# A depthwise convolution on TensorE: 128x128 diagonals replaced by 32x32 diagonals in sixteen tiles of the array

## The chip, the cores and the metric

The kernel runs on one core of one Trainium2 chip. The metric is the device time of one execution in microseconds (us); the figure quoted for a kernel is the median of several runs. TensorE (PE in the profile) has its matmuls and its weight loads (PEld) on separate rows, VectorE is DVE, ScalarE is ACT, GpSimd is POOL, and SP issues the DMAs.

## What is computed

The program is a trunk of four pre-norm residual layers on 256 tokens of 1024 features, in float32. Each layer has a token mixer and a gated feed-forward network (FFN) with a short convolution. The mixers are differential attention (layers 0 and 3), a Conformer convolution module (layer 1) and a gated DeltaNet (layer 2). The change touches the Conformer module and the FFN that stands ahead of it:

```
u = h @ w_in + b_in                       # 1024 -> 2048
a, g = split(u); u = a * sigmoid(g)
u = causal_dwconv(u, dw) + dw_b           # 31 taps, each channel by itself
mu = mean(u); var = mean((u - mu)**2)     # over the 1024 channels
u = (u - mu) * rsqrt(var + 1e-5) * ln_g + ln_b
return silu(u) @ w_out + b_out
```

## The kernel before, in words

Features lie on the 128 partitions and the 256 tokens along the free dimension, so 1024 channels are eight blocks, b = 0 to 7. Weights stream from HBM as units of 128x1024 float32; each unit is split by ACT (`whi`, L173) and DVE (`wlo`, L174) into two float32r halves, and every product with a weight is three float32r matmuls (`mm3`, L282 to L284).

The Conformer module (`conformer`) runs a software pipeline over b. `glu(b)` makes both halves of the gated projection, 48 matmuls of 128x128 by 128x256 into the PSUM tile `pcu`; `glu_act` then has DVE scale them (`cs`, L695), ACT take the sigmoid (`csg`, L697) and DVE form `cu` (L700), the block's convolution input with 30 zero columns ahead of it. `conv(b)` shares out the 31 taps:

- TensorE takes the first 10 (11 in the last block). Each tap is a float32 matmul of a 128x128 diagonal `dg` with the shifted `cu`, which the chip runs as two passes, so 20 matmul instructions of 256 columns in `pcc` (L712). The diagonals are made by ACT (`diag`, L650); `some_diags` puts up to 88 of them into the FFN ahead, four per step of it, and all of the 81 that are needed fit.
- The next six are multiplied by ACT (`ct`, L728) and added by GpSimd into `ya` (L729); from b = 2 on, GpSimd also subtracts the shift `m0` (L731).
- Taps 29 and 30 are ACT's (L724, L725), and the other 13 are DVE's fused multiply-adds (`tap`, L722), accumulated in a PSUM tile `cyp`. Two DVE adds join the parts to `c[:, b]` (L735, L736), and ACT squares the block (L750).

`stat(b)` sums `c` and its square over the channels with TensorE: four passes of a 128x1 weight into `pstat` (L757) for each block, in the middle of the next block's taps. For b = 6 the sums are copied out and turned over to tokens (L763, L765), and for b = 7 they are added token by token (L760). `shift` (L743) takes the mean of block 0 as an early shift, so that the later difference of squares keeps its digits; its matmul stands behind the taps of block 1. After `stat(7)` follow the mean and the reciprocal deviation (L781 to L789), eight activations and the output projection `acc`.

Each engine runs its own instructions in the order that the build put them in. On TensorE that is the order of the calls: glu(b), conv(b - 1), glu(b + 1). On DVE, ACT and GpSimd the work of neighbouring blocks interleaves.

Of the kernel before, what the change touches and what calls it, by code (L numbers as in the profile page):

```python
# [12 lines left out]
ALU = mybir.AluOpType  # L13
# [17 lines left out]
N_RAW = 4  # L31
PE_TAPS = 10
PE_TAPS_LAST = 11
POOL_TAPS = 6
LAG = 2
AT_X, AT_R, AT_S, AT_F, AT_A, AT_C, AT_G = 7, 3, 10, 0, 0, 4, 2
MAX_DIAGS = 88
DIAG_STEP = 4
TAIL = 4
# [42 lines left out]
C_ID, C_LE, C_GT, C_ONE, C_HALF = 0, P, 2 * P, 3 * P, 3 * P + P  # L82
N_CONST = C_HALF + 16

# [41 lines left out]
def trunk(ctx: ExitStack, tc: tile.TileContext, xT, pos, wst, wba, params, consts, rows, lamp, nfin, out, layers=None):  # L126
# [11 lines left out]
    def bank(name="ps"):  # L138
        return wk.tile([P, 512], F32, name=name, tag="wk")
# [55 lines left out]
    neg_half = cst[:, C_HALF:C_HALF + 16]  # L195
    one_col = tri_le[:, P - 1:P]

    def col(name, i):
        c = COLS[name] + i
        return prm[:, c:c + 1]  # L200
# [444 lines left out]

    diags = {}

    def diag(dg, b, j):

        ac.activation(dg, ident, AF.Copy, scale=col("conv_dw", b * 31 + j))  # L650

    def some_diags(pool):

        for n, (b, j) in enumerate((b, j) for b in range(KC) for j in range(pe_taps(b))):
            if n == MAX_DIAGS:
                return
            dg = diags[b, j] = pool.tile([P, P], F32, name=f"dg{b}_{j}")
            diag(dg, b, j)
            if n % DIAG_STEP == DIAG_STEP - 1:
                yield  # L660

    def pe_taps(b):
        return PE_TAPS if b < KC - 1 else PE_TAPS_LAST

    def conformer(after):
        with ExitStack() as es:
# [3 lines left out]
            c = one.tile([P, KC, S], F32, name="cc")  # L670
            pstat = accp.tile([P, 2, 512], F32, name="pstat", tag="acc01")
            psum, ptok = pstat[:, 0], pstat[:, 1]
            m0 = one.tile([P, S], F32, name="m0")
# [3 lines left out]

            def glu(b):
                ps = bank("pcu")
                if b == 0:  # L680
                    pair_proj(ps, nxt(2))
                    norm_stat()
                    us[0] = ps
                    return
                for gv in range(2):
                    feat_proj(ps[:, gv * S:(gv + 1) * S], nxt()[0])
                    if b == 1 and gv == 0:
                        row_bc(rs_tok, rs_bc)
                if b == 1:
                    glu_act(0, us.pop(0))  # L690
                glu_act(b, ps)
# [10 lines left out]

            def conv(b):
                u = us.pop(b)
                npe = pe_taps(b)
                pc = bank("pcc")
                for n, j in enumerate(range(npe)):
                    dg = diags.pop((b, j), None)
                    if dg is None:
                        dg = pool.tile([P, P], F32, name="dg", bufs=6)  # L710
                        diag(dg, b, j)
                    pe.matmul(pc[:, 0:S], dg, u[:, j:j + S], start=(n == 0), stop=(n == npe - 1))  # L712
                    if n == npe - 1 and b == 1:
                        shift()
                    if n == npe // 2 and b > 2:
                        stat(b - 1)
                npo = npe + POOL_TAPS
                ya, yc = (pool.tile([P, S], F32, name=f"cy{n}") for n in range(2))
                acc = accp.tile([P, 2, S], F32, name="cyp", tag=f"acc{2 + b % 2}")

                def tap(j, out, y, op=ALU.add):
                    ve.scalar_tensor_tensor(out, u[:, j:j + S], col("conv_dw", b * 31 + j), y, ALU.mult, op)  # L722

                ac.activation(ya, u[:, 30:], AF.Identity, scale=col("conv_dw", b * 31 + 30), bias=col("conv_dw_b", b))  # L724
                ac.activation(yc, u[:, 29:29 + S], AF.Copy, scale=col("conv_dw", b * 31 + 29))  # L725
                for j in range(npe, npo):
                    t = pool.tile([P, S], F32, name="ct", bufs=3)
                    ac.activation(t, u[:, j:j + S], AF.Copy, scale=col("conv_dw", b * 31 + j))  # L728
                    gp.tensor_tensor(ya, ya, t, ALU.add)  # L729
                if b > 1:  # L730
                    gp.tensor_tensor(ya, ya, m0, ALU.subtract)  # L731
                tap(npo, acc[:, 0], yc)
                for j in range(npo + 1, 29):
                    tap(j, acc[:, 0], acc[:, 0])
                ve.tensor_tensor(yc, acc[:, 0], ya, ALU.add)  # L735
                ve.tensor_tensor(c[:, b], pc[:, 0:S], yc, ALU.add)  # L736
                if b > 1:
                    square(b)

            def shift():  # L740
# [5 lines left out]
            def square(b):  # L746
                if b < 2:
                    ve.tensor_tensor(c[:, b], c[:, b], m0, ALU.subtract)
                sqs[b] = pool.tile([P, S], F32, name="csq", bufs=3)
                ac.activation(sqs[b], c[:, b], AF.Square)  # L750

            def stat(b):

                both = (c[:, b], sqs.pop(b))
                if b < KC - 1:
                    for n, x in enumerate(both):
                        pe.matmul(psum[0:1, n * S:(n + 1) * S], ones_n[:, 0:1], x, start=(b == 0 and n == 0), stop=(b == KC - 2 and n == 1))  # L757
                else:
                    for n in range(4):
                        pe.matmul(ptok[:, n:n + 1], both[n // 2][:, n % 2 * P:(n % 2 + 1) * P], ones_n[:, 0:1], start=False, stop=(n == 3))  # L760
                if b == KC - 2:
                    row = one.tile([1, 512], F32, name="crow")
                    ac.copy(row, psum[0:1])  # L763
                    for n in range(4):
                        pe.matmul(ptok[:, n:n + 1], row[:, n * P:(n + 1) * P], one_col[0:1], start=(n == 0), stop=False)  # L765

            for b in range(KC + 1):
                if b < KC:
                    glu(b)
                if b >= 1:  # L770
                    conv(b - 1)
                if b == 2:
                    square(0)
                    square(1)
                if b == 3:
                    stat(0)
                    stat(1)
            stat(KC - 1)
            tk = one.tile([P, 2], F32, name="ctk")
# [560 lines left out]
    for k, (i, s) in enumerate(layers):  # L1340
        if s:
            extra = iter(())
            if k + 1 < len(layers) and layers[k + 1][0] % 3 == 1 and not layers[k + 1][1]:
                cdiag = ExitStack()
                extra = some_diags(cdiag.enter_context(tc.tile_pool(name="cdiag", bufs=1)))
            ffn(i, after_of(k), extra, k + 1 == len(layers))
# [24 lines left out]
def pack(inp, layers=None):  # L1371
# [100 lines left out]
    cst[:, C_ONE:C_ONE + P] = 1.0 / D  # L1472
    cst[:, C_HALF:] = -0.5

# [27 lines left out]
```

## Time and profile before

| | us |
|---|---|
| median of 3 runs | 1384.86 |
| lowest and highest run | 1383.97, 1385.96 |
| the profiled execution, its own time | 1386.96 |
| its span | 1385.1 |
| PE, DVE, ACT, POOL busy in the span | 1363.5, 1110.9, 879.9, 94.9 |

The profile is one execution. Its own time is 1.9 us more than its span and 2.1 us more than the median. A row of the timeline gives the start, the time from the first start to the last end, the engine, line, operation, output and inputs; in brackets stands the idle time ahead of it and what ended it. Matmuls overlap one another, so the pace of a stream is read from starts, not from the length of one.

### The profile page before, as it was taken

Reading aid. Unit: us, or ns where it says so; the run is one execution under the profiler, and the core shown is the slowest. Engines: PE = TensorE matmul, PEld = TensorE weight load, DVE = VectorE, ACT = ScalarE, POOL = GpSimd, SP = SyncE. Lnnn points to the kernel's source line nnn. Section 1 sums busy time; section 2 is a strip of 40 time slices with the busy share of each in tenths; the row PEclk is TensorE's granted clock in tenths of the full one; section 3 lists DMA queues with packets and bytes.
Section 4 is the critical chain, followed back from the end, with each engine's and each line's share of the span. In section 5 each row is a group of like instructions: output and inputs, shape, how many; then the busy total and the mean of one; then the engine's idle time right before and its main releaser. Section 6 shows DMA issues by size and latency. Waiting matters only on the chain.

```text
span 1385.1 us, 27575 instructions
## 1 busy us (share of the span) xinstructions
PE 1363.5 (98%) x10868; PEld 1292.5 (93%) x10868; DVE 1110.9 (80%) x1994; ACT 879.9 (64%) x1621; POOL 94.9 (7%) x112
## 2 busy tenths in 40 slices
PE   9999999999999999999999999999999999999998
PEld 7889999998889999998989999999999988999996
DVE  7977877788988877787994886797778786787776
ACT  6668965576656555575747765665556576655554
POOL 0010000004530000000100011000000000000000
PEclk9999999999999999999998999999999999999999
DMA  8445666654315666663462333566666544566662
GB/s 281 149 123 158 185 191 188 193 183 122 96 58 171 198 189 192 185 181 122 137 184 91 123 92 110 160 191 185 192 187 184 183 127 133 162 204 186 193 185 91
DMA packets 63138, 223.94 MB, mean 162 GB/s; under 512 B 7200, under 2 KB 8736, under 8 KB 63008
## 3 DMA queue, kind: packets, MB, share of 16 engines
q1 hardware_dynamic: 62720, 221.65, 52.5%
q8 instruction: 85, 1.39, 0.4%
q10 hardware_dynamic: 288, 0.52, 0.1%
q14 instruction: 45, 0.37, 0.1%
HBM read 221.10 MB, written 1.05 MB: 160 GB/s over the span
## 4 chain that ended last, share of the span: by engine, by line
PE 84%; DVE 9%; ACT 4%; POOL 1%; issue 1%; DMA 0%; SPq 0%; POOLq 0%; ACTq 0%; DVEq 0%
PE psu L282 11%; PE psu L283 11%; PE psu L284 11%; PE acc L282 8%; PE acc L283 8%; PE acc L284 8%; DVE wlo L174 3%; PE pgc L282 2%; PE pcc L712 2%; PE pgc L283 2%; PE pgc L284 2%; ACT whi L173 2%; PE pz L282 1%; PE pz L283 1%; PE pz L284 1%
## 5 line engine op out<-in xcount | busy, mean ns | idle before, releaser
L174 DVE TENSOR_TENSOR wlo<-wraw,whi 128x1024 fp32r<-128x1024 f32 (+1 forms) x417 | 508.8, 1222 | 134.6 <-ACT whi L173 132.6
L173 ACT CAST whi<-wraw 128x1024 fp32r<-128x1024 f32 (+1 forms) x417 | 436.0, 1047 | 272.9 <-PE psu L283 105.8
L282 PE MATMUL psu<-xh,whi 128*128 128x256 f32 x1344 | 375.9, 280 | 0.0
L283 PE MATMUL psu<-xl,whi 128*128 128x256 f32 x1344 | 375.2, 279 | 0.0
L284 PE MATMUL psu<-xh,wlo 128*128 128x256 f32 x1344 | 375.1, 279 | 0.0
L282 PEld LDWEIGHTS psu<-xh,whi 128*128 128x128 f32 x1344 | 252.6, 188 | 0.4
L283 PEld LDWEIGHTS psu<-xl,whi 128*128 128x128 f32 x1344 | 252.6, 188 | 0.4
L284 PEld LDWEIGHTS psu<-xh,wlo 128*128 128x128 f32 x1344 | 252.6, 188 | 0.0
L282 PE MATMUL acc<-facth,whi 128*128 128x256 f32 x528 | 147.6, 280 | 0.0
L283 PE MATMUL acc<-factl,whi 128*128 128x256 f32 x528 | 147.3, 279 | 0.0
L284 PE MATMUL acc<-facth,wlo 128*128 128x256 f32 x528 | 146.9, 279 | 0.0
L426 DVE SCALAR_TENSOR_TENSOR fy<-fs,prm,fy 128x255 f32<-128x255 f32 (+1 forms) x352 | 146.4, 477 | 0.0
L422 ACT ACTIVATE fy<-fs,prm 128x256 f32<-128x256 f32 x176 | 96.4, 593 | 8.3 <-DVE fs L418 8.3
L282 PEld LDWEIGHTS acc<-facth,whi 128*128 128x128 f32 x528 | 99.2, 188 | 0.2
L283 PEld LDWEIGHTS acc<-factl,whi 128*128 128x128 f32 x528 | 99.2, 188 | 0.0
L284 PEld LDWEIGHTS acc<-facth,wlo 128*128 128x128 f32 x528 | 99.0, 188 | 0.0
L276 ACT CAST facth<-fa 128x256 fp32r<-128x256 f32 x88 | 35.7, 405 | 93.0 <-DVE fa L430 92.8
L418 DVE TENSOR_TENSOR fs<-psu,rs_bc 128x512 f32<-128x512 f32 x88 | 60.7, 690 | 27.5 <-PE psu L284 26.8
L282 PE MATMUL pqk<-xh,whi 128*128 128x256 f32 x256 | 72.7, 284 | 0.0
L284 PE MATMUL pqk<-xh,wlo 128*128 128x256 f32 x256 | 72.3, 282 | 0.4 <-DVE wlo L174 0.4
L283 PE MATMUL pqk<-xl,whi 128*128 128x256 f32 x256 | 72.4, 283 | 0.0
L282 PE MATMUL pgc<-xh,whi 128*128 128x256 f32 x240 | 69.6, 290 | 0.0
(352 smaller groups left out, 2874.7 us busy)
## 6 DMA issues: line engine op xcount, KB each, us to landing
wraw<-wst SPq DMA_DIRECT2D x415, 512.0 KB, 3.7
h<-xT SPq DMA_DIRECT2D x4, 256.0 KB, 5.0
prm<-params SPq DMA_DIRECT2D x1, 564.0 KB, 7.4
wraw<-wst SPq DMA_DIRECT2D x2, 256.0 KB, 4.0
gain<-nfin SPq DMA_DIRECT2D x1, 512.0 KB, 4.7
out<-fz SPq DMA_DIRECT2D x2, 256.0 KB, 2.0
out<-fz ACTq DMA_DIRECT2D x2, 256.0 KB, 2.5
cst<-consts SPq DMA_DIRECT2D x1, 264.0 KB, 7.5
```

The costliest lines, as they stand in the source:

```text
L173: ac.copy(hi[:, qs], src[:, qs])
L174: ve.tensor_tensor(lo[:, qs], src[:, qs], hi[:, qs].bitcast(F32), ALU.subtract)
L276: state["hi"] = ac.copy(hi, a)
L282: pe.matmul(o, w[0], x[0], start=start, stop=False)
L283: pe.matmul(o, w[0], x[1], start=False, stop=False)
L284: pe.matmul(o, w[1], x[0], start=False, stop=stop)
L418: ve.tensor_tensor(s, ps.rearrange("p (g t) -> p g t", g=2), bc(rs_bc, 2), ALU.mult)
L422: ac.activation(y[:, gv], s[:, gv], AF.Identity, scale=col("ffn_dw", c + 2), bias=col("ffn_dw_b", (i * NP_ + p) * 2 + gv))
L426: ve.scalar_tensor_tensor(y[:, gv, j:], s[:, gv, :S - j], col("ffn_dw", c + 2 - j), y[:, gv, j:], ALU.mult, ALU.add)
L712: pe.matmul(pc[:, 0:S], dg, u[:, j:j + S], start=(n == 0), stop=(n == npe - 1))
```

## The change

TensorE gets 16 taps of each block (20 of the last), GpSimd four in place of six, and DVE nine (five in the last). The diagonal of a tap is kept as four 32x32 diagonals, one for each 32-partition group: `tap_blocks` makes all taps of a block with one GpSimd multiply of a stack of four 32x32 identities (new in `cst`) with the tap columns of `prm`. `some_taps` does that in the FFN ahead, one block at every second step, in place of ACT's 81 diagonals.

A group of four taps runs as 16 small matmuls: row group i of the array reads partitions 32i to 32i+31 of `cu`, column group j holds tap 4r+j, and the result goes to PSUM bank i, partitions 32j to 32j+31. So a bank holds, for 32 channels, four partial sums over taps, one on each partition quarter. ACT copies the four banks to SBUF (`cysb`, three copies), and `join(b)` adds the four quarters by four matmuls with the identity stack, each into one partition quarter of `pcc`. `join(b)` stands between the two halves of glu(b + 2).

DVE's taps accumulate in `yc` in SBUF, since the PSUM banks of `cyp` now hold the partial sums. The sums for the norm over blocks 0 to 6 are made by GpSimd (`total`, two adds a block), and TensorE turns them over to tokens once, after `join(6)`; `join(7)` stands behind that. `shift` moves to `join(0)`.

```diff
-PE_TAPS = 10
-PE_TAPS_LAST = 11
-POOL_TAPS = 6
+PE_TAPS = 16
+PE_TAPS_LAST = 20
+POOL_TAPS = 4
...
-        ac.activation(dg, ident, AF.Copy, scale=col("conv_dw", b * 31 + j))
...
+    def tap_blocks(pool, b):
+
+        n = pe_taps(b)
+        t = taps[b] = pool.tile([P, n, 32], F32, name=f"tp{b}")
+        c0 = COLS["conv_dw"] + b * 31
+        gp.tensor_tensor(t, bc(stack, n), bcl(prm[:, c0:c0 + n], 32), ALU.mult)
+
+    def some_taps(pool):
+
+        for b in range(KC):
+            tap_blocks(pool, b)
+            yield
+            yield
...
             def conv(b):
...
-                    pe.matmul(pc[:, 0:S], dg, u[:, j:j + S], start=(n == 0), stop=(n == npe - 1))
-                    if n == npe - 1 and b == 1:
-                        shift()
-                    if n == npe // 2 and b > 2:
-                        stat(b - 1)
+                hs = slice(b % 2 * S, b % 2 * S + S)
+                for r in range(npe // 4):
+                    for j in range(4):
+                        n = 4 * r + j
+                        for i in range(4):
+                            rows = slice(32 * i, 32 * i + 32)
+                            pe.matmul(y4[i][32 * j:32 * j + 32, hs], tp[rows, n], u[rows, n:n + S], start=(r == 0), stop=(r == npe // 4 - 1))
+                ysb = pool.tile([P, 4, S], F32, name="cysb")
+                ac.copy(ysb[:, 0:2], front[:, :, hs])
+                for q in (2, 3):
+                    ac.copy(ysb[:, q], y4[q][:, hs])
...
-                tap(npo, acc[:, 0], yc)
-                for j in range(npo + 1, 29):
-                    tap(j, acc[:, 0], acc[:, 0])
-                ve.tensor_tensor(yc, acc[:, 0], ya, ALU.add)
+                for j in range(npo, 29):
+                    tap(j, yc)
+                ve.tensor_tensor(yc, yc, ya, ALU.add)
+                store[b] = ysb, yc
+
+            def join(b):
+
+                ysb, yc = store.pop(b)
+                pc = bank("pcc")
+                for i in range(4):
+                    pe.matmul(pc[32 * i:32 * i + 32, 0:S], stack, ysb[:, i], start=True, stop=True)
                 ve.tensor_tensor(c[:, b], pc[:, 0:S], yc, ALU.add)
                 if b > 1:
                     square(b)
+                    if b < KC - 1:
+                        total(b)
+                if b == 0:
+                    shift()
+                if b == 1:
+                    square(0)
+                    square(1)
+                    total(1)
+
+            def total(b):
+
+                for x, y, z in ((c, c[:, b], sums[0]), (sqs, sqs[b], sums[1])):
+                    gp.tensor_tensor(z, (c[:, 0] if x is c else sqs[0]) if b == 1 else z, y, ALU.add)
...
             for b in range(KC + 1):
                 if b < KC:
-                    glu(b)
+                    glu(b, (lambda: join(b - 2)) if b > 1 else (lambda: None))
                 if b >= 1:
                     conv(b - 1)
...
+            join(KC - 2)
+            ptok = bank("ptok")
+            stat(sums, True, False)
+            join(KC - 1)
+            stat((c[:, KC - 1], sqs[KC - 1]), False, True)
```

## Rows read from the trace of the kernel before

**Rows 1.** The page: busy times of the engines over the whole span.
```profile
PE 1363.5 (98%) x10868; PEld 1292.5 (93%) x10868; DVE 1110.9 (80%) x1994; ACT 879.9 (64%) x1621; POOL 94.9 (7%) x112
```

**Rows 2.** Windows, one block of the Conformer: busy us by engine, clock, DMA.
```profile
362.61:373.69 11.08, 11.08 (x75) 9.56 (x73) 10.20 (x22) 6.88 (x13) 6.32 (x9) 1.00 0.34 106
```

**Rows 3.** Timeline of PE in that block, from the end of the projection on.
```profile
368.41 2.75 PE L712 MATMUL pcc<-cu,dg 128*128 128x256 f32 x12
371.09 0.59 PE L757 MATMUL pstat<-cc,cst 128*1 128x256 f32 x2
...
373.69 0.47 PE L282 MATMUL pcu<-xh,whi 128*128 128x256 f32 x1
```

**Rows 4.** Tile views of pcc and psc: duration in ns, min/median/max.
```profile
L712 PE MATMUL pcc<-cu,dg x162: 377/378/484, 324.5 to 402.9; 128*128 128x256 f32 x162
...
L572 PE MATMUL psc<-qkrot x128: 272/375/480, 37.2 to 1160.3; 64*128 64x128 f32 x64, 64*128 64x256 f32 x64
```

**Rows 5.** Timeline of PE, first attention: scores of two heads in two row groups.
```profile
37.15 0.93 PE L572 MATMUL psc<-qkrot 64*128 64x128 f32 x8 [0.46 <-DVE qkrot L554]
```

**Rows 6.** Timeline of PE in the DeltaNet: 32x32 tiles, line after line.
```profile
744.56 2.01 PE L1121 MATMUL pu<-Ls,ysb 32*32 32x32 f32 x61
746.38 0.21 PE L1124 MATMUL pu<-ysb,Ls 32*32 32x32 f32 x1
746.41 0.19 PE L1121 MATMUL pu<-Ls,ysb 32*32 32x32 f32 x1
```

**Rows 7.** DVE's taps: tile view of cyp, and cyp in the block's window.
```profile
L722 DVE SCALAR_TENSOR_TENSOR cyp<-cu,prm,cyp x95: 473/480/491, 326.4 to 401.2; 128x256 f32<-128x256 f32 x95
L722 DVE SCALAR_TENSOR_TENSOR cyp<-cu,prm,cy x8: 486/494/685, 325.9 to 395.1; 128x256 f32<-128x256 f32 x8
...
362.61:373.69 11.08, 6.69 (x17) 1.00 0.34 106
```

**Rows 8.** GpSimd and DVE: tile views of cy and wlo, timelines near 389 us.
```profile
L729 POOL TENSOR_TENSOR cy<-cy,ct x48: 724/737/1624, 326.1 to 399.5; 128x256 f32<-128x256 f32 x48
...
L731 POOL TENSOR_TENSOR cy<-cy,m x6: 722/1164/1678, 345.5 to 400.3; 128x256 f32<-128x256 f32 x6
...
L174 DVE TENSOR_TENSOR wlo<-wraw,whi x417: 691/1224/1571, 6.2 to 1368.3; 128x1024 fp32r<-128x1024 f32 x138, 128x512 fp32r<-128x512 f32 x1
...
388.74 0.74 POOL L731 TENSOR_TENSOR cy<-cy,m 128x256 f32<-128x256 f32 x1
...
388.99 1.57 DVE L174 TENSOR_TENSOR wlo<-wraw,whi 128x1024 fp32r<-128x1024 f32 x1 [0.68 <-ACT whi L173]
```

**Rows 9.** Timeline of the tail, from the last projection to the mean.
```profile
390.61 2.75 PE L712 MATMUL pcc<-cu,dg 128*128 128x256 f32 x12
...
393.52 0.48 DVE L700 SCALAR_TENSOR_TENSOR cu<-cs,prm,csg 128x256 f32<-128x256 f32 x1
...
395.50 4.75 POOL L729 TENSOR_TENSOR cy<-cy,ct 128x256 f32<-128x256 f32 x6 [6.03 <-ACT ct L728]
...
403.36 0.42 DVE L736 TENSOR_TENSOR cc<-pcc,cy 128x256 f32<-128x256 f32 x1 [1.10 <-PE pcc L712]
...
405.21 0.71 PE L789 MATMUL pcm<-cst,ctk 128*128 128x128 f32 x4 [0.32 <-DVE ctk L781]
```

**Rows 10.** Timeline of PE, the first taps of the module.
```profile
324.53 0.67 PE L712 MATMUL pcc<-cu,dg 128*128 128x256 f32 x2 [1.27 <-DVE cu L700]
```

**Rows 11.** Timelines of ACT and PE at the start of the FFN ahead.
```profile
124.80 1.26 ACT L650 ACTIVATE dg<-cst,prm 128x128 f32<-128x128 f32 x4
...
127.79 0.27 PE L298 MATMUL psu<-xh,whi 128*128 128x256 f32 x1
128.71 0.39 PE L299 MATMUL psu<-xl,whi 128*128 128x256 f32 x1 [0.65 <-DVE xl L240]
```

**Rows 12.** Windows in the DeltaNet: busy us by engine, then the granted clock.
```profile
731.00:734.60 3.60, 3.60 (x114) 3.48 (x113) 2.50 (x2) 3.11 (x5) 0.00 (x0) 1.00 0.56 162
734.60:741.40 6.80, 6.80 (x51) 6.74 (x48) 0.70 (x1) 6.07 (x9) 0.00 (x0) 0.50 0.22 72
```

More of the change, by code (lines that the diff above doesn't have):

```diff
@@ L31 @@
 N_RAW = 4
-PE_TAPS = 10
-PE_TAPS_LAST = 11
-POOL_TAPS = 6
+PE_TAPS = 16
+PE_TAPS_LAST = 20
+POOL_TAPS = 4
 LAG = 2
 AT_X, AT_R, AT_S, AT_F, AT_A, AT_C, AT_G = 7, 3, 10, 0, 0, 4, 2
-MAX_DIAGS = 88
-DIAG_STEP = 4
 TAIL = 4
@@ L82 @@
 C_ID, C_LE, C_GT, C_ONE, C_HALF = 0, P, 2 * P, 3 * P, 3 * P + P
-N_CONST = C_HALF + 16
+C_STACK = C_HALF + 16
+N_CONST = C_STACK + 32
 def attn_order():
@@ L196, in trunk @@
     one_col = tri_le[:, P - 1:P]
+    stack = cst[:, C_STACK:C_STACK + 32]
     def col(name, i):
@@ L644, in attn @@
             drive(main, sides, flags)
-    diags = {}
-    def diag(dg, b, j):
-        ac.activation(dg, ident, AF.Copy, scale=col("conv_dw", b * 31 + j))
[L652 to L660, printed above, removed]
+    taps = {}
     def pe_taps(b):
         return PE_TAPS if b < KC - 1 else PE_TAPS_LAST
+    def tap_blocks(pool, b):
[8 more added lines that the diff above has]
+            yield
     def conformer(after):
@@ L670, in conformer @@
             c = one.tile([P, KC, S], F32, name="cc")
-            pstat = accp.tile([P, 2, 512], F32, name="pstat", tag="acc01")
-            psum, ptok = pstat[:, 0], pstat[:, 1]
+            front = accp.tile([P, 2, 512], F32, name="cy4", tag="acc01")
+            y4 = [front[:, q] for q in range(2)]
+            y4 += [accp.tile([P, 512], F32, name="cy4", tag=f"acc{q}") for q in (2, 3)]
+            sums = [one.tile([P, S], F32, name=f"cs{n}") for n in range(2)]
+            store = {}
             m0 = one.tile([P, S], F32, name="m0")
@@ L676, in conformer, with glu @@
             sqs = {}
-            def glu(b):
+            def glu(b, middle):
                 ps = bank("pcu")
@@ L688, in glu @@
                         row_bc(rs_tok, rs_bc)
+                    if gv == 0:
+                        middle()
                 if b == 1:
@@ L705, in conv, with tap @@
                 npe = pe_taps(b)
[L706 to L711, printed above, removed]
-                    pe.matmul(pc[:, 0:S], dg, u[:, j:j + S], start=(n == 0), stop=(n == npe - 1))
-                    if n == npe - 1 and b == 1:
-                        shift()
-                    if n == npe // 2 and b > 2:
-                        stat(b - 1)
+                if b not in taps:
+                    tap_blocks(one, b)
+                tp = taps.pop(b)
+                hs = slice(b % 2 * S, b % 2 * S + S)
[9 more added lines that the diff above has]
+                    ac.copy(ysb[:, q], y4[q][:, hs])
                 npo = npe + POOL_TAPS
                 ya, yc = (pool.tile([P, S], F32, name=f"cy{n}") for n in range(2))
-                acc = accp.tile([P, 2, S], F32, name="cyp", tag=f"acc{2 + b % 2}")
-                def tap(j, out, y, op=ALU.add):
-                    ve.scalar_tensor_tensor(out, u[:, j:j + S], col("conv_dw", b * 31 + j), y, ALU.mult, op)
+                def tap(j, y):
+                    ve.scalar_tensor_tensor(y, u[:, j:j + S], col("conv_dw", b * 31 + j), y, ALU.mult, ALU.add)
                 ac.activation(ya, u[:, 30:], AF.Identity, scale=col("conv_dw", b * 31 + 30), bias=col("conv_dw_b", b))
@@ L748, in square, with stat @@
                     ve.tensor_tensor(c[:, b], c[:, b], m0, ALU.subtract)
-                sqs[b] = pool.tile([P, S], F32, name="csq", bufs=3)
+                sqs[b] = pool.tile([P, S], F32, name="csq", bufs=4)
                 ac.activation(sqs[b], c[:, b], AF.Square)
[L752 to L765, printed above, removed]
+            def stat(both, first, last):
+                for n in range(4):
+                    pe.matmul(ptok[:, n:n + 1], both[n // 2][:, n % 2 * P:(n % 2 + 1) * P], ones_n[:, 0:1], start=(first and n == 0), stop=(last and n == 3))
             for b in range(KC + 1):
                 if b < KC:
-                    glu(b)
+                    glu(b, (lambda: join(b - 2)) if b > 1 else (lambda: None))
                 if b >= 1:
                     conv(b - 1)
[L772 to L778, printed above, removed]
+            join(KC - 2)
[3 more added lines that the diff above has]
+            stat((c[:, KC - 1], sqs[KC - 1]), False, True)
             tk = one.tile([P, 2], F32, name="ctk")
@@ L1344, in trunk @@
                 cdiag = ExitStack()
-                extra = some_diags(cdiag.enter_context(tc.tile_pool(name="cdiag", bufs=1)))
+                extra = some_taps(cdiag.enter_context(tc.tile_pool(name="cdiag", bufs=1)))
             ffn(i, after_of(k), extra, k + 1 == len(layers))
@@ L1472, in pack @@
     cst[:, C_ONE:C_ONE + P] = 1.0 / D
-    cst[:, C_HALF:] = -0.5
+    cst[:, C_HALF:C_STACK] = -0.5
+    cst[:, C_STACK:] = np.tile(np.eye(32), (4, 1))
     rows = np.concatenate([a["gdn_dt_bias"], a["gdn_a_log"]], axis=1)
```

## The prediction

> **What bounds the kernel now.** I read the page's busy times first: TensorE is busy 98% of the span, VectorE 80% [rows 1]. That is an average over stages, so I went to the stage that the change rewrites. The module's convolution runs in equal blocks; in one of 11.08 us TensorE has no idle time, but DVE is busy 10.20 us, with GpSimd at 6.32 and ACT at 6.88 [rows 2]. So TensorE sets the pace here with DVE a microsecond behind it: whatever TensorE gains, DVE returns after 0.9 us a block unless it gets lighter too. Then I read TensorE's own order in that block. The projection takes from 362.61 to 368.41, 5.80 us; taps and sums take 368.41 to 373.69, 5.28 us [rows 2, 3]. One pass of a full diagonal lasts 377 ns by its record, but 12 of them cover 2.75 us, so they follow each other every 0.215 us [rows 3, 4]; ten taps of two passes are 4.3 us, and four passes for sums with two changes of array shape are the other 1.0. A change of shape shows as 371.09 - (368.41 + 2.75 - 0.38) = 0.31 us from start to start in place of 0.215 [rows 3]. Six blocks lie between the first taps at 324.53 and the end of the last projection at 390.61 [rows 9, 10].
>
> **The change, part by part.** All prices below are per block.
>
> *Taps on TensorE.* Sixteen taps in four groups, each 16 tiles of two passes: 128 small matmuls of 256 columns in place of 20 large ones. What a group costs depends on how many tiles run at once, and no row shows sixteen. The bounds: all sixteen together take two passes, 0.43 us a group and 1.7 us a block; only the four row groups together, the column groups in turn, take eight passes, 6.9 us a block. What is shown: two heads' scores in two row groups, eight passes of which four have 128 and four 256 columns, would take 4 x 0.107 + 4 x 0.215 = 1.29 us one after another, and cover 0.93 less a 0.37 tail, 0.56 us [rows 4, 5]. So row groups do run side by side. In the DeltaNet one 32x32 tile takes 61 passes in 2.01 - 0.19 us, one per 0.030 us, and where a second tile takes over, starts of the two lines alternate 0.03 us apart, beside the first line's own [rows 6]: about 0.016 us a pass with two tiles active. I take 128 x 0.016 = 2.1 us, the nearest row with more than one tile active; it lies near the lower bound, and 128 x 0.030 = 3.9 us is my pace-limited case.
>
> By the Trainium skill, TensorE: Matmul & The Clock Gate, Part 3, matmuls start and end strictly in program order and small tiles overlap because they follow one another closely. The trace disagrees with the first half: line 1124 is issued after all of line 1121, and still starts at 746.38, ahead of 1121's start at 746.41 [rows 6]. Had the rule held, the second pass of each tile would hold back every later tile; that is a rival below.
>
> *Join and sums.* The four sum passes go (0.86 us), eight join passes of 32 output columns come: 0.43 us if the four quarters overlap, 1.72 if not; I take 0.5, in line with the taps. Two shape changes more cost 2 x 0.1 plus a slowed first pair, 0.45 us. TensorE's block: 5.80 + 2.1 + 0.5 + 0.45 = 8.9 us.
>
> *DVE.* Thirteen taps become nine. In the block 17 tap instructions occupy 6.69 us, 0.39 each since they overlap [rows 7], so four fewer leave 10.20 - 1.6 = 8.6 us. But the accumulator moves from PSUM to SBUF, and then a tap reads two SBUF operands. The rows show what that does beside GpSimd: taps with one operand in PSUM last 473 to 491 ns whatever GpSimd does; the first tap, whose two operands are both in SBUF, reaches 685 [rows 7]. The weight split, also two SBUF operands, lasts 1.22 us as a rule, but 1.57 when it starts 0.25 us into a GpSimd add of 0.74; and GpSimd's own add goes from 0.73 to 1.6 when the split is ahead of it [rows 8]. So the two wait for each other, by 0.19 to 0.35 us on DVE's side. GpSimd will have seven adds a block: four taps, the shift, two sums. I charge 7 x 0.27 = 1.9 us, the middle of the two delays, and get 10.5 us for DVE. Ends: nothing (8.6), and the whole time that the row shows an add to hold the port, 0.25 + 0.35 = 0.60 us each, 12.8.
>
> So the block falls from 11.08 to 10.5, DVE and GpSimd now setting it: 6 x 0.6 = **-3.5 us**. ACT loses two taps and gains three copies at 6.88/13 = 0.53 each [rows 2]; it stays under 8 us and waits for nobody's sake. The DMA queue runs at a third of its share [rows 2], and nothing new is put on it but 32 columns of constants.
>
> *Tail.* Now 14.60 us pass from the last projection to the mean, and c of block 7 is ready at 403.36, when its 22 passes and the sums ahead of them are through [rows 9]. After: u of block 7 at 394.0 as now [rows 9], 160 small passes 2.6 us, three copies 1.6, join(6) in their shadow, then c and its square 0.9, two GpSimd adds 1.5, stat and join(7) about 1.1, while GpSimd's chain (now 395.50 to 400.25, six adds) also needs its sums in. That gives c(7) near 401.5 to 402, **-1.5**. The queue behind the new wait is TensorE's: stat waits for GpSimd's last sum, and join(7) stands behind stat. In series with paced tiles this is 404.6, +1.3; without GpSimd on the path -3.
>
> *The shift.* Its matmul moves to join(0), ahead of half a projection. c(0) needs nine taps in sequence from 324.53: about 1.1 for ACT, 4.7 to 5.8, adds 0.8, so 331 to 332.4, while TensorE reaches it at 324.53 + 2.1 + 2.9 + 0.5 = 330.0. Bounds 0 (if other work is put ahead) and +2.4; I take **+1.0**.
>
> *The FFN ahead.* 81 diagonals leave ACT. The stage is bound by TensorE, and only at its start do they show: four of them, 1.26 us at 124.80, hold up ACT, and TensorE waits 0.92 us at 127.79 for a normalised input instead of 0.12 [rows 11]. Worth up to 0.8; GpSimd's eight products of 512 elements (at most twice a 0.74 add each) may stall DVE's splits once there. I take **-0.4**, between -0.8 and +0.4.
>
> Sum: -3.5 - 1.5 + 1.0 - 0.4 = -4.4 us on the profiled execution, whose own time of 1386.96 becomes 1382.6; the median of the runs is 2.1 lower, so **1380.5**. The runs of before differ by 0.14%; under 0.2%, 2.8 us, I call it no change.
>
> **The rivals.**
> - *The tiles overlap and the collisions hardly count.* The block is TensorE's 8.9: 6 x 2.2 = -13, and -0.9 of the rest: 1371. For it: most delays in rows 8 fall on GpSimd, which has time. Against: nine taps in a row leave it few gaps.
> - *DVE and GpSimd become the bound (slower).* Each of seven adds holds a dense row of taps back for its 0.60: 12.8 us a block, 6 x 1.7 = +10.3, less 0.9: 1394. It decides as soon as DVE's collisions exceed 11.08 - 8.6 = 2.5 us a block, 0.35 for each add, the longest delay that a row shows.
> - *The same with whole adds.* If an add held the port for its full 0.74 us, DVE's block would be 8.6 + 5.2 = 13.8 us, 6 x 2.7 = +16.3, less 0.9: 1400. The row's 0.60 speaks against it [rows 8]. This is the rule of the Trainium skill, SBUF — State Buffer, in its section on the two separate sides: whichever of the two starts first keeps the shared port for the whole instruction.
> - *TensorE is paced by issue.* 3.9 us of taps, join at 1.07 (between its bounds): 5.80 + 3.9 + 1.07 + 0.45 = 11.2, as now; tail +1.3, shift +1.0, FFN -0.4: 1387.5. For it: 0.030 us is the only steady pace shown [rows 6].
> - *Column groups take turns,* so the change doesn't do what it says: 5.80 + 6.9 + 1.7 + 0.45 = 14.9, 6 x 3.8 = +22.6; in the tail 6.9 and 8.6 us of taps put c(7) at 413, +9.5: 1417.
> - *Strict order.* Each tile's second pass waits 0.215 and all behind it: 64 x 0.215 = 13.8 us of taps, a block of 20.5, 6 x 9.4 = +57, tail about +22: 1464. Rows 6 speak against it.
> - *The clock.* It fell to half after a stretch of 32x32 passes and stayed there 6.8 us [rows 12], a loss of 3.4. Once in each of eight blocks: +27 less 4.4, 1408. Against: sixteen tiles of 256 columns between full projections are far from one tile of 32.
>
> **How the numbers follow.** Forecast 0.46 (its own range 1376 to 1384.5); no collisions 0.12; collisions 0.12, with whole adds 0.02; paced 0.13; turns 0.08; strict order 0.03; clock 0.04. The range reaches over forecast, no collisions, collisions and paced: 1370 to 1396, leaving out 0.17 above. Faster by over 0.2% (under 1382.1): 0.12 and four fifths of 0.46, 0.50. Within 0.2% (to 1387.6): the rest of the forecast and most of the paced case, 0.19. Slower: 0.31.
>
> **What would show it.** In the changed profile the block is from one projection's start to the next's: about 10.5 us, TensorE with gaps of a microsecond and a half, ended by DVE. The small taps: 128 in about 2.1 us from first to last start; 3.5 to 4 means pace, near 7 turns. DVE's taps: a median over 0.48 and a maximum near 1 show collisions. The last join waiting for GpSimd's sum shows the tail. I am wrong if TensorE still has no gaps in the block, or if taps of DVE don't lengthen.

## The result and the profile after

The changed kernel takes 1420.32 us (median of 4 runs, 1418.34 to 1421.49) against 1385.11 us (1383.97 to 1385.96): a ratio of 1.0244, interval 1.0231 to 1.0258. I had forecast 1380.5 with a range of 1370 to 1396. The profiled execution took 1421.21 us with a span of 1419.3.

Where the time went, by stage. Each length is the difference between the starts of the first TensorE matmuls of two stages in the timelines; the middle column is a second profile of the kernel before, described at the end of the experiments.

| us | before | before, again | after |
|---|---|---|---|
| until the FFN ahead | 123.6 | 125.4 | 125.6 |
| FFN ahead of the module | 187.0 | 187.0 | 196.2 |
| module, first projection to the mean (pcm) | 94.7 | 94.7 | 112.3 |
| the mean to the output projection | 3.9 | 5.4 | 6.4 |

So 26.8 us lie in two places, +9.2 in the FFN and +17.6 in the module. The module splits once more. From its first projection to the taps of block 1 it takes 321.85 to 354.68, 32.8 us, where before it was 310.55 to 334.53, 24.0. Five blocks follow, to 414.26: 59.6 us instead of 56.1. The tail, to the mean at 434.11, is 19.85 us instead of 14.60 [rows 9].

The page's busy times, beside [rows 1]:

```profile
PE 1373.5 (97%) x11798; PEld 1297.9 (91%) x11798; DVE 1120.8 (79%) x1959; ACT 856.3 (60%) x1547; POOL 106.3 (7%) x116
```

TensorE's busy time rose by 10.0 us, although its taps became cheaper; part of that is the granted clock, as the next view shows. Windows of four blocks, each from one run of small taps to the next (length, then busy us of PE, PEld, DVE, ACT, POOL, then granted clock, DMA share, GB/s), beside [rows 2]:

```profile
364.82:379.28 14.46, 11.41 (x185) 9.49 (x184) 12.07 (x20) 6.86 (x15) 5.81 (x9) 0.88 0.24 74
379.28:389.94 10.66, 9.88 (x186) 7.98 (x185) 9.30 (x13) 6.22 (x12) 6.92 (x8) 1.00 0.35 102
389.94:403.63 13.69, 11.39 (x185) 9.10 (x184) 12.13 (x19) 6.96 (x15) 7.76 (x9) 0.88 0.25 78
403.63:414.26 10.63, 9.86 (x185) 7.97 (x184) 9.28 (x13) 6.23 (x12) 6.84 (x7) 1.00 0.33 101
```

In [rows 2] TensorE had no idle time. Here **no engine is busy throughout**: in the block of 14.46 us TensorE has 3.05 us free and DVE 2.39. On the mean of the four, DVE is busy 10.70 us (42.78 / 4) and the block lasts 12.36 (49.44 / 4). In the two long blocks the granted clock is 0.88: by that mean it was at 0.5, the lower of the two levels, for 3.3 to 3.5 us of each, and TensorE had stood before it fell.

The long block, engine by engine. PE's timeline shows the taps, beside [rows 3], and the join:

```profile
364.82 2.76 PE L722 MATMUL cy<-cu,tp 32*32 32x256 f32 x128
...
373.65 1.20 PE L751 MATMUL pcc<-cysb,cst 128*32 128x256 f32 x8 [3.05 <-ACT cysb L724]
```

The 128 small passes take 2.76 us, 0.021 each, and are over at 367.6. The join that needs their copies starts 6 us later, after 3 us in which TensorE did nothing. ACT's timeline says why:

```profile
370.39 0.60 ACT L733 ACTIVATE cy<-cu,prm 128x256 f32<-128x256 f32 x1 [1.28 <-DVE cu L705]
370.90 0.49 ACT L734 ACTIVATE cy<-cu,prm 128x256 f32<-128x256 f32 x1
371.29 1.83 ACT L737 ACTIVATE ct<-cu,prm 128x256 f32<-128x256 f32 x4
373.04 0.57 ACT L724 COPY cysb<-cy 128x512 f32<-128x512 f32 x1
```

In ACT's queue, as the program was built, the ya, yc and four ct of the **next** block (L733, L734, L737) stand ahead of the copies of **this** one (L724). They need that block's u; so the copies, whose taps are through at 367.6, wait for DVE. And DVE is late, because its taps got longer (timelines of DVE, with u in its first line, and of GpSimd):

```profile
369.87 0.48 DVE L705 SCALAR_TENSOR_TENSOR cu<-cs,prm,csg 128x256 f32<-128x256 f32 x1
371.42 6.49 DVE L731 SCALAR_TENSOR_TENSOR cy<-cu,prm,cy 128x256 f32<-128x256 f32 x9 [1.07 <-ACT cy L734]
```
```profile
371.86 3.33 POOL L738 TENSOR_TENSOR cy<-cy,ct 128x256 f32<-128x256 f32 x4 [3.04 <-ACT ct L737]
375.27 0.79 POOL L740 TENSOR_TENSOR cy<-cy,m 128x256 f32<-128x256 f32 x1
```

Nine taps last 6.49 us while GpSimd makes its four adds and the shift's subtraction. The tile views of both, beside [rows 7, 8]:

```profile
L731 DVE SCALAR_TENSOR_TENSOR cy<-cu,prm,cy x68: 467/831/951, 337.2 to 423.3; 128x256 f32<-128x256 f32 x68
```
```profile
L738 POOL TENSOR_TENSOR cy<-cy,ct x32: 724/791/904, 337.4 to 423.1; 128x256 f32<-128x256 f32 x32
```

The median tap takes 831 ns, where [rows 7] had 480. GpSimd's add goes only from 737 to 791.

DVE also loses time without working: its nine taps wait for ACT's yc, which waits for u, and nothing else of DVE's queue stands in between, so it is idle for 1.07 us ahead of each run of taps. The chain of work that ended last goes this way in these blocks (pieces of it, from the start of a split to the first tap):

```profile
380.50 1.13 DVE wlo L173
381.64 0.88 DVE cu L705
382.54 0.60 ACT cy L733
383.57 0.49 DVE cy L731
```

From one run of nine taps to the next it is 12.15 us (371.42 to 383.57), then 12.20 and 12.15: DVE busy 10.7, 1.07 for yc, 0.4 in pauses of hundredths. The copies are on that chain at 360.08 and 421.79, not between. So in these blocks DVE sets the pace, and TensorE's wait for the copies runs beside it.

The waits of the module (who waited for whom, us, times, longest):

```profile
PEld pcc L751 <- ACT cysb L724: 10.9, 6, 3.3
...
PEld cy L722 <- POOL cy L738: 5.8, 1, 5.8
...
PEld pm L772 <- DVE cc L752: 4.8, 1, 4.8
```

The first is the join waiting for the copies, six times. The second is conv(7), which this view puts down to GpSimd and TensorE's timeline to the copies of block 6. The third is the shift's matmul. In the tail, beside [rows 9]:

```profile
414.26 2.76 PE L722 MATMUL cy<-cu,tp 32*32 32x256 f32 x128
422.36 5.19 PE L722 MATMUL cy<-cu,tp 32*32 32x256 f32 x160 [5.34 <-ACT cysb L724]
427.48 0.64 PE L751 MATMUL pcc<-cysb,cst 128*32 128x256 f32 x8
429.46 0.61 PE L784 MATMUL ptok<-cst,cs 128*128 128x1 f32 x4 [1.35 <-POOL cs L767]
```

Last, the FFN ahead, beside [rows 11] (timelines of GpSimd, DVE and PE):

```profile
125.91 11.41 POOL L656 TENSOR_TENSOR tp<-cst,prm 128x512 f32<-128x512 f32 x8 [12.71 <-PE acc L284]
```
```profile
126.46 2.47 DVE L240 SCALAR_TENSOR_TENSOR xl<-h,prm,xh 128x256 fp32r<-128x256 f32 x2
128.85 1.54 DVE L251 TENSOR_TENSOR sqacc<-sqacc,sq 128x512 f32<-128x512 f32 x1
```
```profile
131.58 0.38 PE L298 MATMUL psu<-xh,whi 128*128 128x256 f32 x1 [1.56 <-ACT xh L239]
133.61 0.58 PE L299 MATMUL psu<-xl,whi 128*128 128x256 f32 x1 [1.65 <-DVE xl L240]
137.75 0.98 PE L270 MATMUL psn<-cst,sqacc 128*128 128x1 f32 x4 [1.43 <-DVE sqacc L253]
```

All eight tables run back to back in the stage's first 12 us, though the code yields between them: nothing else is in GpSimd's queue, so it runs ahead. That is just where DVE makes TensorE's normalised input, and TensorE waits three times, 4.6 us together; from 132.3 its clock is at the lower level for 10.24 us. TensorE works for 7.50 of these, so about 3.7 us are lost.

### The profile page after: what moved, and what is told of

It reads as the page before. It is cut to its first block, busy times and chain, and to the rows that moved or that the text cites. A ratio compares the mean times of both kernels' runs of the same rounds, so it can differ in the third digit from the quotient of the medians.

```text
span 1419.3 us, 29304 instructions
## 1 busy us (share of the span) xinstructions
PE 1373.5 (97%) x11798; PEld 1297.9 (91%) x11798; DVE 1120.8 (79%) x1959; ACT 856.3 (60%) x1547; POOL 106.3 (7%) x116
## 4 chain that ended last, share of the span: by engine, by line
PE 79%; DVE 13%; ACT 4%; issue 2%; POOL 1%; DMA 0%; SPq 0%; POOLq 0%; ACTq 0%; DVEq 0%
PE psu L282 11%; PE psu L283 11%; PE psu L284 11%; PE acc L282 8%; PE acc L283 7%; PE acc L284 7%; DVE wlo L173 4%; DVE cy L731 2%; PE pgc L282 2%; PE pgc L283 2%; PE pgc L284 2%; ACT whi L172 1%; PE pz L282 1%; PE pz L284 1%; PE pz L283 1%
```

## The experiments

My theory after this: three causes. The tables delay the FFN. In the module GpSimd's adds stretch DVE's taps (collisions), and the queues' order lets TensorE feel it (order). Rivals: the small tiles cost more than they seem; the shift's new place is what holds TensorE; only one of collisions and order counts. For the kernel before, taken beside the experiments, the times are 1389.1 (one run), 1388.99 and 1388.36 us (medians).

**The tables on DVE.**

```diff
-        gp.tensor_tensor(t, bc(stack, n), bcl(prm[:, c0:c0 + n], 32), ALU.mult)
+        ve.tensor_tensor(t, bc(stack, n), bcl(prm[:, c0:c0 + n], 32), ALU.mult)
```

> The eight tables of taps are made by DVE instead of GpSimd; nothing else changes. Port theory (GpSimd's products and DVE's two-operand work hold each other up in the FFN ahead): TensorE's three waits of 1.8 to 2.0 us at the start of that FFN go, the FFN falls from 196.2 us to about 187, and the run by about 9 us to 1411. Rival (the waits come from the missing ACT work or from the order of the weights): FFN stays within 2 us of 196.

1411.36 us; the FFN takes 187.4 us, the module 112.3 as before. DVE's timeline at the place of the collisions:

```profile
126.14 0.88 DVE L240 SCALAR_TENSOR_TENSOR xl<-h,prm,xh 128x256 fp32r<-128x256 f32 x2
126.93 0.69 DVE L251 TENSOR_TENSOR sqacc<-sqacc,sq 128x512 f32<-128x512 f32 x1
...
128.14 0.69 DVE L656 TENSOR_TENSOR tp<-cst,prm 128x512 f32<-128x512 f32 x1
```

The two xl take 0.88 us instead of 2.47, and a table on DVE takes 0.69 us where GpSimd needed 1.43 (11.41 / 8). So the tables' place on GpSimd cost most of the 8.8 us, through DVE. Not all of it: from 160 to 280 us TensorE makes 342 passes in 40 us in the changed kernel and 345 here, with no wait in either, which is 1.6 us in this FFN. Three runs below have the tables on GpSimd and 345 passes; their FFN takes 194.2 to 195.5 us, 6.8 to 8.1 more than here. What sets the two paces stays open.

**DVE's taps accumulate in PSUM again.**

```diff
+                acc = bank("cyp")[:, 0:S]
-                    ve.scalar_tensor_tensor(y, u[:, j:j + S], col("conv_dw", b * 31 + j), y, ALU.mult, ALU.add)
+                    ve.scalar_tensor_tensor(acc, u[:, j:j + S], col("conv_dw", b * 31 + j), y, ALU.mult, ALU.add)
-                    tap(j, yc)
-                ve.tensor_tensor(yc, yc, ya, ALU.add)
+                    tap(j, yc if j == npo else acc)
+                ve.tensor_tensor(yc, acc, ya, ALU.add)
```

> DVE's taps accumulate in a PSUM bank again, in place of SBUF; GpSimd's adds stay. Port theory: the taps that last 0.85 us beside GpSimd fall to 0.49, a run of nine from 6.5 to about 4.7 us, and the module from the first projection to the mean falls from 112.3 us by 6 to 10. Order theory (TensorE waits for ACT's copies, which stand behind the next block's activations in ACT's queue): taps get shorter too, but the waits ahead of the joins stay, and the module falls by less than 3.

1402.39 us, module 93.6: 18.7 us less, nearly twice the most that I had expected. The tile view of the taps:

```profile
L733 DVE SCALAR_TENSOR_TENSOR cyp<-cu,prm,cyp x60: 475/490/491, 336.5 to 403.4; 128x256 f32<-128x256 f32 x60
L733 DVE SCALAR_TENSOR_TENSOR cyp<-cu,prm,cy x8: 483/696/942, 336.0 to 400.6; 128x256 f32<-128x256 f32 x8
```

Taps with one operand in PSUM keep to 490 ns beside the same adds; the eight that still read two SBUF operands go up to 942. This shows the collisions. It doesn't give their price alone, since the build now also mixes taps of two blocks with the weight splits on DVE, where the changed kernel has nine taps in one run. ACT's copies still stand behind the next block's ct here, and the joins still wait for them, but only 0.25 to 0.52 us in four blocks.

**Copies first on ACT.**

```diff
-                    ac.copy(ysb[:, q], y4[q][:, hs])
+                    copied = ac.copy(ysb[:, q], y4[q][:, hs])
+                before, store["copied"] = store.get("copied"), copied
...
+                with following(before):
+                    ac.activation(ya, u[:, 30:], AF.Identity, scale=col("conv_dw", b * 31 + 30), bias=col("conv_dw_b", b))
```

So ya, yc and the four ct of block b are queued behind the copies of block b - 1; GpSimd's adds stay.

> An order on ACT alone: the copies of a block's partial sums stand ahead of the next block's own taps. Order theory: TensorE's waits ahead of the joins (2.8, 3.3, 1.1, 2.6 and 1.0 us) and inside the last block's taps (5.7) go, and the module falls from 112.3 us by 10 or more. Port theory: the waits move to DVE's work, whose taps still last 0.85, and the module falls by less than 4.

1401.53 us, module 96.2: 16.1 us less, with the collisions still there:

```profile
L732 DVE SCALAR_TENSOR_TENSOR cy<-cu,prm,cy x68: 470/616/961, 335.6 to 407.8; 128x256 f32<-128x256 f32 x68
```

So order is worth nearly as much, but not ACT's alone. This edit, too, changes DVE's order in the build: a block's taps now lie between other work, DVE no longer stands for yc, and in the block from 364.76 on it is busy 10.19 of 10.44 us. No run changes ACT's queue by itself.

**The shift where it was.**

```diff
+                if b == 1:
+                    shift()
                 ysb = pool.tile([P, 4, S], F32, name="cysb")
```

> The matmul of the shift stands behind the taps of block 1 again, in place of right behind join(0). If TensorE's wait of 4.9 us there and the half clock after it are the shift's doing, the module falls from 112.3 us by 5 to 8; if the wait is only the first sign of a late DVE, it moves to the next join and the module falls by less than 2.

1419.48 us, module 110.2. The wait of 4.8 us at the shift's matmul goes, but the join of block 1 waits 3.0 us instead. The gain of 2.1 us lies between the two expectations, next to the second. So the shift's place is at most a small part; c of block 0 is late whoever waits for it.

**No adds on GpSimd, all queues as they are.**

```diff
-                    gp.tensor_tensor(ya, ya, t, ALU.add)
-                if b > 1:
-                    gp.tensor_tensor(ya, ya, m0, ALU.subtract)
```

> Leaves out the four adds of GpSimd in each block (ct into ya) and the subtraction of m0 from ya, so these parts of the sum are missing; ACT still makes the four ct and the order of every engine's queue stays as in the changed kernel (nine taps of DVE in one run, ACT's copies behind the four ct of the next block). Port theory (GpSimd's adds stretch DVE's taps, and that alone is what the accumulator in PSUM took away): the taps fall from 0.85 us in a run to 0.50, the module from 112.3 us to 93 to 97, the time to 1402 to 1406. Order theory (the accumulator in PSUM gained because the build then interleaved DVE's taps with other work; the order of the queues alone holds TensorE): taps of 0.50 us, but a module of 105 to 110 us and 1413 to 1418.

The kernel leaves these parts of the sum out. 1406.88 us, module 99.6: 12.7 us less, between the two expectations, so neither alone is right. Here DVE's and ACT's queues have the order of the changed kernel, so this is the price of GpSimd's instructions by themselves. Nearly all of it is collisions: the waits for GpSimd that go with them are small in the changed kernel, 0.9 us of ACT (for the buffers of ct) and 0.6 of DVE (for the sum) in the whole module. One run of nine taps, from DVE's timeline, and a join of that block:

```profile
361.84 4.65 DVE L731 SCALAR_TENSOR_TENSOR cy<-cu,prm,cy 128x256 f32<-128x256 f32 x9 [1.07 <-ACT cy L734]
```
```profile
363.93 1.15 PE L748 MATMUL pcc<-cysb,cst 128*32 128x256 f32 x8 [1.18 <-ACT cysb L724]
```

6.49 - 4.65 = 1.84 us for five instructions of GpSimd, 0.37 each. And the join still waits for the copies. Now they are on the chain that ended last:

```profile
373.82 0.48 ACT cysb L724
...
374.34 1.15 PE pcc L748 x8
```

It goes round from u over ya, yc, the four ct, the copies and the join to half a projection, and back over the weight split to u: 10.41 us in the block from 368.04. So ACT's order holds these blocks 1.1 us over TensorE's own 9.3 (next), and in the changed kernel DVE's 12.2 us hide it.

**No adds and copies first.** Both edits together.

> Leaves out GpSimd's four adds in each block and the subtraction of m0, as the run without adds did, and puts ACT's ya, yc and ct of a block behind the copies of the block before it. It is the fourth corner beside the changed kernel (module 112.3 us), the run without adds alone (99.6) and the run with the copies first alone (96.2). If the collisions and the queue order are two causes that add, the module comes to 112.3 - 12.7 - 16.1 = 83.5 us, which is under what TensorE's own work allows, so at most to about 88 us, as with all four repairs. If they are one loop and either repair breaks it, the module stays at 94 to 97 us. Time 1394 to 1397 in the first case, 1400 to 1405 in the second (the tables stay on GpSimd in both).

1392.98 us, module 86.8. With that there is a table of four for the module:

| module, us | copies behind the next block's ct | copies first |
|---|---|---|
| GpSimd's adds as they are | 112.3 | 96.2 |
| without the adds | 99.6 | 86.8 |

("Copies first" includes what the build then changes in DVE's order; the table doesn't tell ACT's queue from DVE's.) Without adds the order is worth 12.8 us, with them 16.1; with the copies first the adds cost 9.4, else 12.7. They nearly add up; with both, TensorE's own work sets the block:

```profile
345.19:354.47 9.28, 9.28 (x186) 7.72 (x185) 9.07 (x18) 6.54 (x14) 1.49 (x2) 1.00 0.28 97
```

**The order of the sixteen tiles.**

```diff
-                    for j in range(4):
-                        for i in range(4):
+                    for i in range(4):
+                        for j in range(4):
```

> The sixteen tiles of a group of taps in the other order: the four column tiles of one row group after each other, row groups outside. If all sixteen tiles run at once and the pace is that of issue, the order makes nothing: 128 passes again in 2.6 to 2.8 us from first to next, 1418 to 1422. If tiles that share a row group hold each other up (their moving data comes in on the same rows), the 128 passes take 3.5 to 6.9 us and the module grows by 6 to 30 us: 1426 to 1450.

1419.29 us, and from PE's timeline:

```profile
364.53 2.76 PE L722 MATMUL cy<-cu,tp 32*32 32x256 f32 x128
```

Not a hundredth of a us between the two orders, so the row groups don't hold each other up at this pace.

**All four repairs, and three without the shift.**

> All four repairs together: tables on DVE, taps of DVE accumulating in PSUM, ACT's ya, yc and ct of a block behind the copies of the block before it, the shift back behind the taps of conv(1). The FFN ahead takes 187 to 188 us in any case. If collisions and queue order are two causes that add, the module falls from 112.3 us to 87 to 90 and the time to 1386 to 1389, no more than 0.3% over the kernel before. If they are one loop that either repair breaks, the module stays at 92 to 95 and the time is 1390 to 1394. If the blocks come down to TensorE's 8.9 us throughout, the module is 84 to 86 and the time 1382 to 1385, at or under the kernel before.

> As the run with all four repairs, but the shift stays at join(0). If TensorE's wait there for c of block 0 is a cost of its own (2.8 to 4.9 us of gaps in the changed kernel, of which moving it back alone brought 2.1), the module is 2 to 3 us longer than with all four. If the wait only moves with c(0), both are within 0.7 us of each other.

1388.17 us with all four (ratio to before 0.9991, interval 0.9980 to 1.0001; module 88.4) and 1388.01 with the shift left at join(0) (0.9994, 0.9981 to 1.0006; module 88.0). Both are level with the kernel before, and the shift's place is worth nothing. Windows of the run with four repairs: six blocks, then the tail to the mean:

```profile
328.60:384.60 56.00, 56.00 (x1106) 46.66 (x1106) 53.07 (x91) 40.01 (x83) 37.50 (x44) 1.00 0.34 110
384.60:403.09 18.49, 12.71 (x321) 8.59 (x321) 12.63 (x24) 8.90 (x19) 9.38 (x12) 0.85 0.18 59
```

TensorE has no idle time for six blocks, 9.33 us each, at the full clock; in the kernel before the same stretch was 390.61 - 324.53 = 66.08 us [rows 9, 10]. So the change does save 10 us in the blocks, once nothing holds TensorE up. Of these, 3.9 go again in the tail, 18.49 us instead of 14.60. Outside the module, the FFN takes 189.1 us in both runs, over the 187 to 188 expected and 2.1 over the kernel before: TensorE makes 342 passes in 40 us there, as in the changed kernel. In the tail:

```profile
390.83 5.38 PE L722 MATMUL cy<-cu,tp 32*32 32x256 f32 x160 [3.47 <-DVE cu L705]
...
398.13 0.61 PE L788 MATMUL ptok<-cst,cs 128*128 128x1 f32 x4 [1.35 <-POOL cs L771]
```

The cheaper taps of block 6 no longer cover the time in which DVE makes u of block 7.

**The tail reordered.** On top of the four repairs:

```diff
+                if b == KC:
+                    join(KC - 2)
                 if b >= 1:
                     conv(b - 1)
-            join(KC - 2)
+            square(KC - 2)
             stat(sums, True, False)
+            stat((c[:, KC - 2], sqs[KC - 2]), False, False)
```

(GpSimd's sums end with block 5; DVE's taps of block 6 are queued behind the product of u's gating input for block 7. A second version has 24 of block 7's taps on TensorE.)

> All four repairs, and the tail reordered: the join of block 6 ahead of conv(7), GpSimd's running sums end with block 5 and TensorE sums block 6 itself, DVE's taps of block 6 stand behind the gating product of block 7. If the 18.5 us of the tail were order alone (3.8 us of conv(7) waiting for u of block 7, 2.7 us of sums waiting for GpSimd, and the half clock that the gaps brought), the tail is 11 to 14 us, no half clock in it, 4 us from the mean to the next stage instead of 6.0: 1379 to 1383, faster than the kernel before by 0.4 to 0.7%. If the waits only change places (the weight splits of DVE still ahead of u, GpSimd's four adds of block 7 last), the tail stays at 16 to 18 us and the time at 1385 to 1388.

> As the run with the tail reordered, with 24 of block 7's taps on TensorE in place of 20: four taps of DVE (2.0 us) go, 32 more passes at 0.021 us (0.7 us) come. If DVE's taps end the tail, it is 0.5 to 1.3 us shorter than with 20. If TensorE or GpSimd's adds end it, it is 0 to 0.8 us longer.

1384.01 us, ratio 0.9971, interval 0.9959 to 0.9982: faster than the kernel before by 0.3%. That is less than the 1379 to 1383 us expected, and the tail lies between the two cases, as its length below shows. The module takes 85.9 us. From PE's timeline:

```profile
388.70 0.59 PE L722 MATMUL cy<-cu,tp 32*32 32x256 f32 x2 [1.40 <-DVE cu L705]
...
397.52 0.61 PE L789 MATMUL ptok<-cst,cc 128*128 128x1 f32 x4 [1.50 <-DVE cc L759]
```

The tail is 15.88 us (383.01 to 398.89), the wait for GpSimd's sums is gone and most of the half clock with it; but u of block 7 is still 1.4 us late, behind a weight split. With 24 taps the tail is 16.48 us (384.27 to 400.75), 0.6 longer, so DVE's taps don't end it; the time is 1383.37 us, 0.9973 (0.9960 to 0.9986), which can't be told from the other.

**The kernel before, profiled again.**

> The kernel before, unchanged, profiled beside the experiments. In its profile of earlier the FFN ahead of the module starts at 123.6 us; in the changed kernel and in all experiments at 125.1 to 125.6. If these 1.5 to 2 us come from the change (its constants are 32 columns longer), the FFN starts at 123.4 to 123.8 here too; if they belong to the conditions of these runs, in which the kernel before takes 1388 to 1389 us in place of 1385, it starts at 125.0 to 125.8. The module is 94 to 95.5 us, and 3.8 to 4.2 us from the mean to the next stage, in either case.

1391.74 us. Its FFN starts at 125.43, so the 2 us ahead of the FFN belong to the conditions of the runs, not to the change; and from the mean to the output projection it takes 5.4 us, not the 4 I expected, with the clock at the lower level from 408.2 to 411.6. Against this profile (span 1389.9) the changed kernel is 29.4 us longer, of which 26.8 are the FFN and the module. What differs between the conditions stays open.

## Why the prediction was wrong

**TensorE's terms were nearly right.** Taps 2.1 us forecast, 2.69 from first to next start in the unhindered blocks (0.021 us a pass, between my 0.016 and 0.030); join and changes of shape 0.95, and what a block of 9.26 us leaves for them is 9.26 - 5.80 - 2.69 = 0.77. The whole block of 8.9 us is 9.26 to 9.33. Strict order (13.8 us of taps), turns of the column groups (6.9) and pace (3.9) are refuted by that row, and turns by the order of the tiles too: its 1417 us is near the result for a reason that isn't there. The clock's rival fails as well: in six blocks of small tiles without a gap the granted clock is 1.00. Where it fell, TensorE had been waiting.

**The step that failed** is the one from busy times to the block: "So the block falls from 11.08 to 10.5, DVE and GpSimd now setting it", and beside it "ACT ... stays under 8 us and waits for nobody's sake". DVE's busy time was forecast at 10.5 and measures 10.70; the block is 12.36. I took the busiest engine's sum for the length, as if every engine could work ahead. That holds only while no queue puts one block's work behind another's.

DVE does set the block, but with pauses that my sum had at nothing: 12.15 to 12.20 us from run to run, of which 1.07 are its wait for ACT's yc. In the kernel before, two taps of another block lie in that place and DVE waits only 0.21 us (at 372.74); here the nine stand in one run behind yc. ACT, too, is on TensorE's path, because the join needs its copies in the middle of the next projection, and ACT's queue has them behind six instructions that need DVE's u. I counted ACT's 6.88 us and never asked in which order they stand. The two queues' order together is 13 to 16 us of the module. How much of it is ACT's alone is not shown; in the run without adds its path holds a block at 10.41 us, against 9.3 for TensorE's own work.

By size: the six blocks and the shift were forecast at -2.5 us and measure +12.4 (335.82 to 414.26, 78.44 us instead of 66.08), the FFN is 9.6 us off, the tail 6.75. So this step is the largest of three.

**The collisions** were seen, and their total sized about right: the four blocks' DVE is busy 10.70 us, two blocks without adds 8.89 (17.78 / 2 by their windows), so 1.8 us a block for five instructions. The two sums, which that run keeps, add about 0.5 in three of the four blocks, where u takes 0.95 us instead of 0.48. That is 2.2 to 2.3 against my 7 x 0.27 = 1.9. Two errors hide in it. In a run of taps each of GpSimd's instructions costs 0.37, just over the upper delay of [rows 8]. And a tap costs 0.52 from start to start when all nine are one chain (4.65 - 0.485 = 4.17 over eight), not the 0.39 that I read where two chains and other work were mixed. By the Trainium skill, SBUF — State Buffer, section on the two separate sides, whichever of the two starts first keeps the shared port for the whole instruction. The trace agrees that they delay each other, but not with the size: one tap and one add together take 0.52 + 0.37 = 0.89 us, less than the two lengths of 0.49 and 0.79 after each other. The rivals of collisions named the right engines, but their 1394 and 1400 us leave out what the order of the queues adds.

**The FFN ahead:** -0.4 forecast, +9.2 measured, of which 6.8 to 8.1 are the tables and 1.6 the slower passes. I had the eight products and wrote that they "may stall DVE's splits once there". I took the yields for a spread in time. A yield orders the instructions as they are issued; GpSimd had nothing else to do and ran them at once.

**The shift:** +1.0 forecast, +8.8 to the taps of block 1. My reckoning of c(0) had its nine taps at 5.8 us at most and nothing for the order of the queues. In DVE's queue c(0), at 349.37, stands behind all eighteen taps of blocks 0 and 1, which run from 337.20 to 348.92. By its timeline TensorE waits 2.53 us at join(0) for ACT's copies and 4.48 at the shift, and the granted clock is 0.50 to 0.52 from 344.5 to 354.4. Moving the shift back gave 2.1 us, and with the other repairs nothing.

**The tail:** -1.5 forecast, +5.25 measured; with all collisions and queues repaired it is still +3.9. I took u of block 7 "at 394.0 as now". That is 3.4 us after the last projection; in the changed kernel u ends at 419.0, 4.75 after it, and conv(7) then waits for block 6's copies until 422.36. With the queues repaired, the copies are out of the way and TensorE waits for u, which stands behind a weight split and, until the last repair, the taps of block 6.

## What to carry to other kernels

A sum of busy times bounds a block only from below. When work moves to another engine, write down for each queue in which order the instructions of two neighbouring blocks stand, and follow the new edges (here: u, ACT's yc, DVE's taps; and TensorE's taps, ACT's copy, join) through them; put what TensorE waits for first. And an engine that looks free, as GpSimd at 7% here, is not free of charge: its instructions lengthened those of DVE that read two operands from SBUF, so keep DVE's accumulator in PSUM where a bank is left, and check where in the stage an idle engine will really run.

## What was not expected of the hardware

Sixteen 32x32 tiles of TensorE take a pass of 256 columns every 0.021 us in either order of the tiles: 128 passes in 2.76 us, where one after another by the 0.215 us of [rows 3] they would take 27.5. GpSimd's product of a 128x512 table takes 1.43 us beside DVE, DVE's own 0.69. In this module the granted clock fell to the lower level after waits of TensorE of 2.53, 4.48, 3.05 and 2.30 us; through six blocks of small tiles without a wait it stayed at the full one. TensorE's stream of full passes in the FFN ran at 342 passes in 40 us in some profiles and at 345 in others, both at a granted clock of 1.00.
